# Feed-forward of an encoder trunk: when the activations' forms are cut, how early plain weights are begun, and which engine makes the activations' low halves

## The chip, the cores and the metric

One Trainium2 chip, one of its cores. The core has TensorE (PE: matrix products; PEld is its loading of the stationary operand), VectorE (DVE), ScalarE (ACT), GpSimd (POOL) and SyncE (SP), which issues most transfers. Each engine works through its own instructions in the order in which they were written; semaphores let one engine wait for another. The metric is device time of one execution in microseconds. The kernel before takes 1579.46 us (median of three runs, 1577.26 to 1580.77).

## The reference

Two layers of an encoder on 512 tokens of 1024 channels, in float32. The attention half of a layer (latent attention, grouped-query attention, pooling, gates) is untouched by the change. The feed-forward half is:

```python
hf = rms_norm(x, ffn_norm_g[l])
u = depthwise_conv(hf @ ffn_w_up[l], ffn_conv_w[l], ffn_conv_b[l])   # width 3, along the tokens
u_gate, u_val = u[..., :D_FF], u[..., D_FF:]                         # D_FF = 2816
x = x + (jax.nn.silu(u_gate) * u_val) @ ffn_w_down[l]
```

## The kernel before, in words

**Three products for one.** Every matrix is held as a rounded high half (type fp32r) and a low half, the rest. `mm3` makes a product of three matmuls: high by high, high by low, low by high. So everything that PE reads has to be cut into two halves first: ACT copies the value into the high tile, and the low tile is the value less the high one.

**How a low half is made.** For plain weights of the feed-forward ("u", line 436) and for the forms "11", "12" and "22" the function `by_transfer` does it: ACT writes the high half (`wh`, `fh`) and its negative (`wl`, `fl`), and a transfer on POOL's queue adds the raw weight to that. For the other forms, and for the activations' forms, DVE subtracts. For the finished activation of a chunk (`ah`/`al`, or `HH`/`HL` where the tile is kept in the place of the normalised input) the subtraction was POOL's (line 1675).

**The feed-forward's chunks.** The 2816 hidden channels are 22 chunks of 128 channels, each with a gate part and a value part, in groups of 6, 5, 4, 4 and 3 (`SIZES`). The first group (chunks 0 to 5) is computed plainly: 12 units, of 24 matmuls of 512 columns each. The other chunks go by a scheme with seven products in place of eight, on halves of the tokens and four-way splits of the inputs: per chunk seven forms in the order 11, 12, 1, 22, 2, 4, 3 (`FORMS`), each 12 matmuls of 256 columns (four input pieces q, by three). After the forms 22, 2, 4 and 3 stand matmuls of the down projection of earlier groups ("d", into `ps_mi` and `ps_S`). Each form needs its own combination of weights (`w_form`) and of the normalised input. The input's combinations are built once a layer by `build_forms`, during the plain chunks: eight normalised tiles `hn`, of them four times four sums `tt` (`sums`), and of `hn` and `tt` six sets of four tiles `tf` (`cut`), each one ACT copy (high) and one DVE subtraction (low). The tiles `tf` stay for all sixteen chunks of the layer.

**What sets the order.** One program text writes all engines. A clock (`Clock`) goes forward with each matmul written; a `chain` is a list of steps, each written when the clock's estimate says that the one before is done. So the order on DVE, ACT and POOL follows from when a step came due in that estimate, not from any priority on the chip. Before, the eight `hn` and the four `sums` are one chain without pause, and the `tf` come in two chains beside each other:

```python
chain(*[lambda k=k: normed(k) for k in range(KC)], *[lambda q=q: sums(q) for q in range(4)], after=0.0)
for names in (("11", "1", "2"), ("12", "22", "3")):
    chain(*[z for name in names for q in range(4) for z in cut(name, q)], after=0.3)
```

**When weights are begun.** `wnext` gives PE's next piece of weights, and ahead of that begins the cutting of pieces `n` further on: `LA` = 3 among plain pieces, `LAF` = 6 near forms. Raw weights come by SP's queue into tiles of 1024 columns for a pair of pieces, or, for the four inputs of a form, into single slots ("alone"). `room` says how many of each kind may be held at once: 3 pairs and 8 alone. A new transfer is written when a tile comes free (`w_free`).

**The end of a chunk.** `convolve` takes the finished `u`: an ACT step with scale and bias (`a<-u,prm`), two DVE steps for the neighbours (`a<-u,prm,a`), for the gate part a Silu on ACT (`a<-a,a` on DVE for the product with the value part), then the cut into high and low.

Of the kernel before, what the change touches and what calls it, by code (L numbers as in the profile page):

```python
# [19 lines left out]
T = 512  # L20
D = 1024
KC = D // P
# [10 lines left out]
RAW = 3  # L33
ALONE = 8
# [5 lines left out]
MID = 5  # L40
PRE_A = 16
PRE_B = 8
LA, LAF = 3, 6
SIZES = (6, 5, 4, 4, 3)
PLACE = {1: 0, 2: 5, 3: 0}
KEEP = 2
FORMS = ("11", "12", "1", "22", "2", "4", "3")
SPOTS = ("22", "2", "4", "3")
END = object()
# [142 lines left out]
class Clock:  # L192
# [37 lines left out]
    def done(self, *key):  # L230
        self.ready[key] = self.fin + self.SEM
# [7 lines left out]
    def has(self, *keys):  # L239
        return all(self.ready.get(k, 1e9) <= self.now for k in keys)  # L240

    def chain(self, *steps, after=0.2):

        def go(n, source=None):
            if n == len(steps):
                return
            keys, fn = steps[n] if isinstance(steps[n], tuple) else ((), steps[n])
            late = [self.ready.get(k, self.now + 0.5) for k in keys]
            if late and max(late) > self.now:
                self.at(max(late) - self.now, lambda: go(n))  # L250
                return
            self.fin, self.source, self.last = self.now, source, None
            fn()
            source, self.source = self.last, None
            self.at(max(0.0, self.fin - self.now), lambda: go(n + 1, source))
        self.at(after, lambda: go(0))

    def drain(self):
# [63 lines left out]
def trunk(ctx: ExitStack, tc: tile.TileContext, x, w, prm, gb, cst, out):  # L322
# [3 lines left out]
    at, need, done, chain = ck.at, ck.need, ck.done, ck.chain  # L326
    V, A, G = Engine(ck, nc.vector, "DVE"), Engine(ck, nc.scalar, "ACT"), Engine(ck, nc.gpsimd, "Pool")
# [54 lines left out]
    st = {"dma": 0, "split": 0, "use": 0, "ffn": False}  # L382
    raws, halves, second = {}, {}, {}
    kinds = [2 if i < KC else int(a) for i, a in enumerate(alone)]
    held, room = [0, 0, 0], (RAW, ALONE, KC)

    def w_dma():
        i = st["dma"]
# [6 lines left out]
    def w_until(i):  # L395
        while st["dma"] <= min(i, len(swidth) - 1):
            w_dma()
# [52 lines left out]
    def w_form(j, form, pi):  # L450


        sl = [pieces[pi + n][0] for n in range(4)]
        w_until(sl[3])
        a11, a12, a21, a22 = (raws[i][:, :T] for i in sl)
        ck.fin = ck.now
        if form in ("11", "12", "22"):
            hi, lo = halves[j] = pair(j, True)
            by_transfer(hi[:, :T], lo[:, :T], {"11": a11, "12": a12, "22": a22}[form])
            done("w", j)  # L460
            return
        hi, lo = halves[j] = pair(j)
        if form == "2":
            second[pi] = slot("s2")[:, :T]
        s2 = second.get(pi)
        dst, x, y, op, keys, gone = {
            "1": (a21, a21, a22, ALU.add, [], None),
            "2": (s2, a21, a11, ALU.subtract, [("sum", pi, "1")], 0),
            "4": (a12, a12, s2, ALU.subtract, [("sum", pi, "2")], None),
            "3": (s2, a22, s2, ALU.subtract, [("sum", pi, "4"), ("form", pi, "2")], 3)}[form]  # L470

        def total():
            V.tensor_tensor(dst, x, y, op)
            done("sum", pi, form)
            if gone is not None:
                w_free(sl[gone])

        def low():
            V.tensor_tensor(lo[:, :T], dst, f(hi[:, :T]), ALU.subtract)
            done("w", j)  # L480
            done("form", pi, form)
            if form == "4":
                w_free(sl[1])
            if form == "2":
                w_free(sl[2])

        chain((keys, total), lambda: A.activation(hi[:, :T], dst, AF.Copy), low, after=0.0)
# [10 lines left out]

    def wnext():
        j = st["use"]  # L500
        n = LAF if any(units[min(i, len(units) - 1)][0] not in "pu" for i in (j, j + LAF)) else LA
        w_ahead(j + n if j > LA else j)
        st["use"] += 1
        need(("w", j))
        return halves.pop(j)
# [35 lines left out]
    def split(hi, lo, src, scale=None, eng=None):  # L541

        steps = []
        if scale is None:
            steps.append(lambda: A.activation(hi, src, AF.Copy))
            steps.append(lambda: (eng or V).tensor_tensor(lo, src, f(hi), ALU.subtract))
        else:
            steps.append(lambda: A.activation(hi, src, AF.Copy, scale=scale))
            steps.append(lambda: V.scalar_tensor_tensor(lo, src, scale, f(hi), ALU.mult, ALU.subtract))
        return steps  # L550
# [116 lines left out]
    def layer(l, sq, xsrc):  # L667
# [927 lines left out]
        def build_forms():  # L1595
            for q in range(4):
                m = mp.tile([P, 3, T], F32R, tag="m", name=f"tf{l}{q}")
                forms["raw", q] = m
                for n, name in enumerate(("11", "12", "4")):
                    forms[name, q] = m[:, n, :]  # L1600
                for name in ("1", "22", "2", "3"):
                    forms[name, q] = slot("tf", F32R)[:, :T]
            hn, tt = {}, {}
            lo, hi = slice(0, 256), slice(256, 512)

            def normed(k):
                hn[k] = slot("hn")[:, :T]
                V.scalar_tensor_tensor(hn[k], XM[:, k, :], col(PRM_FG + k), fin["rbc"][:, :T], ALU.mult, ALU.mult)
                done("hn", l, k)

            def sums(q):
                a, b = hn[2 * q], hn[2 * q + 1]
                t = tt[q] = (slot("tt")[:, :T], slot("tt")[:, :T])
                V.tensor_tensor(t[0][:, lo], a[:, hi], a[:, lo], ALU.subtract)
                V.tensor_tensor(t[1][:, lo], b[:, hi], a[:, hi], ALU.subtract)
                V.tensor_tensor(t[0][:, hi], b[:, hi], t[0][:, lo], ALU.subtract)
                V.tensor_tensor(t[1][:, hi], b[:, lo], t[0][:, hi], ALU.subtract)
                done("tt", l, q)

            def cut(name, q):  # L1620
                n = "tt"
                if name == "11":
                    src, dh, dl, n = lambda: hn[2 * q][:, lo], forms[name, q][:, lo], forms[name, q][:, hi], "hn"
                elif name == "12":
                    m = forms["raw", q]
                    src, dh, dl, n = (lambda: hn[2 * q + 1].rearrange("p (a b) -> p a b", a=2)), m[:, 1:3, lo], m[:, 1:3, hi], "hn"
                else:
                    i, h = {"1": (0, lo), "2": (0, hi), "3": (1, lo), "22": (1, hi)}[name]
                    src, dh, dl = lambda: tt[q][i][:, h], forms[name, q][:, lo], forms[name, q][:, hi]

                def low():
                    V.tensor_tensor(dl, src(), f(dh), ALU.subtract)
                    done("tf", l, name, q)
                    if name == "12":
                        done("tf", l, "4", q)
                key = ("tt", l, q) if n == "tt" else ("hn", l, 2 * q + (name == "12"))
                return [([key], lambda: A.activation(dh, src(), AF.Copy)), low]

            chain(*[lambda k=k: normed(k) for k in range(KC)], *[lambda q=q: sums(q) for q in range(4)], after=0.0)
            for names in (("11", "1", "2"), ("12", "22", "3")):  # L1640
                chain(*[z for name in names for q in range(4) for z in cut(name, q)], after=0.3)

        chain(([("rbc", G2)], build_forms), after=3.0)

# [10 lines left out]
        def convolve(c, part, u):  # L1655
            ci = c + part * FC
            a = slot("a")
            steps = [
                lambda: A.activation(a[:, :T], u[:, :T], AF.Identity, bias=col(PRM_B + ci),
                                     scale=col(PRM_W1 + ci)),  # L1660
                lambda: V.scalar_tensor_tensor(a[:, 1:T], u[:, 0:T - 1], col(PRM_W0 + ci), a[:, 1:T],
                                               ALU.mult, ALU.add),
                lambda: V.scalar_tensor_tensor(a[:, 0:T - 1], u[:, 1:T], col(PRM_W2 + ci), a[:, 0:T - 1],
                                               ALU.mult, ALU.add)]
            if part == 0:
                def gate():
                    A.activation(a[:, :T], a[:, :T], AF.Silu)
                    gated[c] = a
                    done("gate", l, c)
                return steps + [gate]  # L1670
            ah, al = act[c] = keep_act(c)

            def prod():
                V.tensor_tensor(a[:, :T], a[:, :T], gated.pop(c)[:, :T], ALU.mult)
            return steps + [([("gate", l, c)], prod), *split(ah, al, a[:, :T], eng=G), lambda: done("act", l, c)]

        def plain(c, part):
            n = 2 * c + part
# [328 lines left out]
```

## Time and profile before

| | |
|---|---|
| median of the runs | 1579.46 us |
| profiled execution | 1578.39 us |
| its span | 1576.6 us |
| PE busy | 1548.2 us, 98% |
| DVE, ACT, POOL busy | 70%, 66%, 55% |

How to read a profile line: a start and a duration in us, the engine, the source line, the operation, then what is written and what is read by the program's names (`wl<-raw`), partitions x elements. In brackets stands the idle time of that engine just before, and what ended it. In a table of windows the columns are: the window and its length, then for PE, PEld, DVE, ACT and POOL the busy time and in brackets the number of instructions, then the granted TensorE clock (1.00 is full), the share of the transfer engines' time (it can come out above 1) and GB/s. The plain stage of the first layer runs from 432.45 us to 502.81 us, the first chunk with forms (chunk 6) follows it. The second layer repeats this 781.3 us later.

### The profile page before, as it was taken

What the parts mean: (1) busy time and instruction counts of PE and PEld (TensorE: products, weight loads), DVE (VectorE), ACT (ScalarE), POOL (GpSimd) and SP (SyncE); (2) the same over time, 40 slices, a digit from 0 to 9 for tenths busy, and PEclk for the clock granted to TensorE, in tenths of its full rate; (3) what the DMA queues carried; (4) which work ended last, traced back from release to release, by engine and by line L of the source; (5) the groups of instructions that cost most, each with busy time, mean ns of one, the idle gap of its engine ahead of it and who ended that gap; (6) DMA issues with size and microseconds to landing.
All of it is one profiled execution on the core that took longest, in us unless ns stands there. A gap on an engine that the chain in (4) does not pass through costs nothing.

```text
span 1576.6 us, 23997 instructions
## 1 busy us (share of the span) xinstructions
PE 1548.2 (98%) x8193; PEld 1338.6 (85%) x8193; DVE 1111.4 (70%) x1816; ACT 1034.4 (66%) x1932; POOL 859.7 (55%) x868
## 2 busy tenths in 40 slices
PE   9999989999999999999999999899999999999999
PEld 8888878888877999998888888788888779999987
DVE  6867886875278777777656688778652877777774
ACT  5557776763478777777655587666535787777773
POOL 3974876854653433333588658668546443333333
PEclk9999999999999999999999999999999999999999
DMA  5432224324489887886535322343244798888853
GB/s 205 126 114 74 74 85 144 107 67 134 113 179 230 200 193 185 205 183 132 135 117 141 100 74 74 96 138 101 70 146 123 170 229 192 192 198 187 194 113 101
DMA packets 127563, 222.36 MB, mean 141 GB/s; under 512 B 29648, under 2 KB 51664, under 8 KB 127440
## 3 DMA queue, kind: packets, MB, share of 16 engines
q1 hardware_dynamic: 90864, 162.93, 33.2%
q0 software_dynamic: 31680, 57.69, 21.3%
q8 instruction: 64, 1.05, 0.3%
q10 hardware_dynamic: 4896, 0.21, 0.2%
q14 instruction: 59, 0.48, 0.1%
HBM read 149.41 MB, written 13.63 MB: 103 GB/s over the span
## 4 chain that ended last, share of the span: by engine, by line
PE 74%; DVE 13%; ACT 6%; issue 4%; POOL 2%; DMA 1%; SPq 0%; ACTq 0%; DVEq 0%; POOLq 0%
PE ps_acc L508 32%; PE ps_AV L508 14%; PE ps_ST L508 12%; PE ps_S L508 8%; PE ps_mi L508 8%; DVE a L294 2%; DVE XM L290 2%; ACT wh L283 1%; DVE wl L290 1%; DVE u L290 1%; DVE mgl L290 1%; ACT mgh L283 1%; DVE hn L294 1%; ACT fh L283 1%; DVE tf L290 1%
## 5 line engine op out<-in xcount | busy, mean ns | idle before, releaser
L290 POOL TENSOR_TENSOR wl<-raw,wh 128x512 fp32r<-128x512 f32 (+3 forms) x241 | 305.0, 1275 | 224.6 <-ACT wh L283 206.5
L283 ACT ACTIVATE wh<-raw 128x512 fp32r<-128x512 f32 (+2 forms) x457 | 269.2, 605 | 56.9 <-DVE raw L290 12.9
L421 POOL DMA_DIRECT2D wl<-raw x124 | 110.9, 919 | 290.3 <-ACT wl L283 106.0
L508 PE MATMUL ps_acc<-HH,wl 128*128 128x512 f32 x416 | 164.3, 395 | 6.2 <-DMA wl<-raw 6.2
L508 PE MATMUL ps_acc<-HH,wh 128*128 128x512 f32 x416 | 164.1, 394 | 3.4 <-DVE vm L290 2.9
L294 DVE SCALAR_TENSOR_TENSOR a<-u,prm,a 128x511 f32<-128x511 f32 x176 | 142.8, 811 | 32.2 <-ACT a L283 31.2
L508 PE MATMUL ps_acc<-HL,wh 128*128 128x512 f32 x416 | 163.5, 393 | 0.0
L421 POOL DMA_DIRECT2D fl<-raw x96 | 85.2, 887 | 105.7 <-ACT sx L283 47.0
L290 DVE TENSOR_TENSOR wl<-raw,wh 128x512 fp32r<-128x512 f32 (+2 forms) x93 | 92.4, 995 | 60.6 <-ACT wh L283 60.5
L283 ACT ACTIVATE a<-u,prm 128x512 f32<-128x512 f32 x88 | 71.5, 815 | 86.6 <-DVE u L290 86.2
L298 DVE TENSOR_REDUCE nm<-ps_S 128x1 fp32r<-128x512 f32 x128 | 87.6, 685 | 36.0 <-PE ps_S L508 34.8
L508 PEld LDWEIGHTS ps_acc<-HH,wl 128*128 128x128 f32 x416 | 78.8, 189 | 24.9 <-DMA wl<-raw 7.9
L508 PEld LDWEIGHTS ps_acc<-HH,wh 128*128 128x128 f32 x416 | 79.0, 190 | 19.8 <-issue 4.4
L508 PE MATMUL ps_AV<-tf,wh 128*128 128x256 f32 x512 | 94.8, 283 | 0.0
L508 PE MATMUL ps_acc<-tf,wh 128*128 128x256 f32 x512 | 94.4, 282 | 0.0
L508 PE MATMUL ps_ST<-tf,fh 128*128 128x256 f32 x512 | 94.2, 281 | 0.0
L508 PEld LDWEIGHTS ps_acc<-HL,wh 128*128 128x128 f32 x416 | 78.9, 190 | 16.3
L508 PEld LDWEIGHTS ps_acc<-tf,wh 128*128 128x128 f32 x512 | 83.9, 191 | 5.3
L508 PEld LDWEIGHTS ps_AV<-tf,wh 128*128 128x128 f32 x512 | 81.4, 190 | 2.6
L283 ACT ACTIVATE wl<-wh 128x512 fp32r<-128x512 f32 x124 | 78.5, 633 | 3.9
L508 PEld LDWEIGHTS ps_ST<-tf,fh 128*128 128x128 f32 x512 | 79.4, 190 | 0.0
L508 PE MATMUL ps_acc<-tf,wl 128*128 128x256 f32 x256 | 72.4, 283 | 0.0
(417 smaller groups left out, 4844.8 us busy)
## 6 DMA issues: line engine op xcount, KB each, us to landing
raw<-w SPq DMA_DIRECT2D x162, 512.0 KB, 3.7
raw<-w SPq DMA_DIRECT2D x136, 256.0 KB, 4.2
wl<-raw POOLq DMA_DIRECT2D x124, 256.0 KB, 4.3
fl<-raw POOLq DMA_DIRECT2D x96, 256.0 KB, 5.4
raw<-w SPq DMA_DIRECT2D x14, 384.0 KB, 3.0
XM<-x SPq DMA_DIRECT2D x16, 256.0 KB, 3.2
dtq<-tr SPq DMA_DIRECT2D x16, 192.0 KB, 1.9
dtk<-tr SPq DMA_DIRECT2D x16, 192.0 KB, 2.0
```

Of the source, the lines that this page charges most:

```text
L283: return self.eng.activation(out, in_, func, **k)
L290: return self.eng.tensor_tensor(out, *a)
L294: return self.eng.scalar_tensor_tensor(out, *a)
L298: return self.eng.tensor_reduce(out, in_, *a, **k)
L421: nc.gpsimd.dma_start(f(lo), r, accum_op=ALU.add)
L508: PE.matmul(o, lhsT=lhsT, rhs=rhs, start=start, stop=stop, skip_group_check=again)
```

## The change

Four edits, none of which changes a value that is computed:

- `build_forms`: `hn` and `tt` are now built four times in the row hn, hn, sums, with at least 1.9 us between the starts of steps (`PACE_H`), and the `tf` in one chain in the order in which PE uses them (11, 12, 1, 22, 2, 3), with at least 1.0 us between steps (`PACE_F`). A step is one ACT copy or one DVE subtraction.
- `wnext`: between plain pieces of the feed-forward, cutting begins 4 pieces ahead (`LAP`) in place of 3.
- `room`: at first, and until a form comes up within the next 24 units, 4 alone raws may be held in place of 8. (One chunk's forms use four.)
- `convolve`: the low half of an activation is POOL's for chunks 0 to 4 and DVE's from chunk 5 on, 17 in each layer.

```diff
-LA, LAF = 3, 6
+LA, LAP, LAF = 3, 4, 6
+PACE_H, PACE_F = 1.9, 1.0
@@ class Clock
-    def chain(self, *steps, after=0.2):
+    def chain(self, *steps, after=0.2, pace=0.0):
...
-            self.at(max(0.0, self.fin - self.now), lambda: go(n + 1, source))
+            self.at(max(pace, self.fin - self.now), lambda: go(n + 1, source))
@@ trunk
-    held, room = [0, 0, 0], (RAW, ALONE, KC)
+    held, room = [0, 0, 0], [RAW, 4, KC]
@@ w_form
         sl = [pieces[pi + n][0] for n in range(4)]
+        room[1] = ALONE if any(u[0] not in "pu" for u in units[j + 1:j + 24]) else 4
         w_until(sl[3])
@@ wnext
-        n = LAF if any(units[min(i, len(units) - 1)][0] not in "pu" for i in (j, j + LAF)) else LA
+        kinds_ = [units[min(j + i, len(units) - 1)][0] for i in (0, LAP, LAF)]
+        n = LAF if any(k not in "pu" for k in kinds_) else LAP if "u" in kinds_[:2] else LA
@@ build_forms
-            chain(*[lambda k=k: normed(k) for k in range(KC)], *[lambda q=q: sums(q) for q in range(4)], after=0.0)
-            for names in (("11", "1", "2"), ("12", "22", "3")):
-                chain(*[z for name in names for q in range(4) for z in cut(name, q)], after=0.3)
+            chain(*[z for q in range(4) for z in (lambda q=q: normed(2 * q), lambda q=q: normed(2 * q + 1), lambda q=q: sums(q))],
+                  after=0.0, pace=PACE_H)
+            chain(*[z for name in FORMS if name != "4" for q in range(4) for z in cut(name, q)], after=0.3, pace=PACE_F)
@@ convolve
-            return steps + [([("gate", l, c)], prod), *split(ah, al, a[:, :T], eng=G), lambda: done("act", l, c)]
+            return steps + [([("gate", l, c)], prod), *split(ah, al, a[:, :T], eng=G if c < SIZES[0] - 1 else V), lambda: done("act", l, c)]
```

The orders of PE and of SP stay the same, row for row. Three places on the other engines, with the rows as they stand in the two programs (numbers behind a name tell tiles of one name apart; they differ between the programs):

ACT, first layer, inside chunk 6, where PE works on its forms 1, 22 and 2; `fh` and `fl` are chunk 7's first weight forms. Before, no `tf` stands here, since all are cut:

```order
L283 ACTIVATE wh_5353<-s_824_5281 128x512
L283 ACTIVATE wh_5376<-raw_5208 128x512
L283 ACTIVATE wl_5377<-wh_5376 128x512
L283 ACTIVATE sx_5307<-ps_AV_5352 128x256
L283 ACTIVATE ah_5302<-a_5301 128x512
L283 ACTIVATE fh_5395<-raw_5210 128x512
```

Now (`tf_4744` and `tf_4749` are the pieces q = 2 and 3 of form 2, `tf_4735` is q = 0 of form 3):

```order
L284 ACTIVATE wl_5364<-wh_5363 128x512
L284 ACTIVATE tf_4744<-tt_4929 128x256
L284 ACTIVATE sx_5294<-ps_AV_5340 128x256
L284 ACTIVATE ah_5289<-a_5288 128x512
L284 ACTIVATE fh_5384<-raw_5166 128x512
L284 ACTIVATE fl_5385<-fh_5384 128x512
L284 ACTIVATE sx_5294<-ps_ST_5362 128x256
L284 ACTIVATE fh_5399<-raw_5168 128x512
L284 ACTIVATE fl_5400<-fh_5399 128x512
L284 ACTIVATE tf_4749<-tt_4990 128x256
L284 ACTIVATE tf_4735<-tt_4793 128x256
```

The last piece of form 2 is now cut five rows behind the place of the first `fh`, in the chunk whose own form 2 reads it.

DVE a little further on, where the first sum of down products has to be added to `XM`. Before:

```order
L290 TENSOR_TENSOR s_849_5468<-raw_5214,raw_5210 128x512
L290 TENSOR_TENSOR XM<-ps_mi_5400,XM 128x512
L294 TENSOR_SCALAR a_5452<-u_5304,prm_91,a_5452 128x511
L290 TENSOR_TENSOR wl_5467<-s_849_5468,wh_5466 128x512
L290 TENSOR_TENSOR u_5305<-ps_acc_5308,sx_5307 128x256
```

Now (`tf_4745` and `tf_4750` are the pieces q = 2 and 3 of form 3):

```order
L291 TENSOR_TENSOR XM<-ps_mi_5389,XM 128x512
L295 TENSOR_SCALAR a_5446<-u_5291,prm_91,a_5446 128x511
L291 TENSOR_TENSOR tf_4745<-tt_4930,tf_4745 128x256
L291 TENSOR_TENSOR wl_5463<-s_849_5464,wh_5462 128x512
L295 TENSOR_SCALAR a_5446<-u_5291,prm_91,a_5446 128x511
L291 TENSOR_TENSOR tf_4750<-tt_4991,tf_4750 128x256
```

Two low halves that PE's form 3 reads now stand behind the step that waits for the last matmul ahead of form 3 (`XM<-ps_mi`).

POOL in chunk 18 of the first layer, before: the low half of that chunk's activation stands behind two transfers of weights.

```order
L421 DMA wl_7952<-raw_7599 128x512
L421 DMA fl_7998<-raw_7713 128x512
L421 DMA fl_8018<-raw_7737 128x512
L290 TENSOR_TENSOR HL<-a_7913,HH 128x512
L421 DMA fl_8058<-raw_7793 128x512
```

Now it is DVE's:

```order
L291 TENSOR_TENSOR a_7914<-a_7914,a_7877 128x512
L291 TENSOR_TENSOR wl_7975<-s_1126_7894,wh_7974 128x512
L291 TENSOR_TENSOR HL<-a_7914,HH 128x512
L291 TENSOR_TENSOR raw_7769<-raw_7769,raw_7795 128x512
L291 TENSOR_TENSOR wl_8032<-raw_7769,wh_8031 128x512
```

It follows the product that it cuts by one row, and stands ahead of the next chunk's first sum of weights.

## The prediction

> **What bounds the kernel.** I read the page first (busy shares), then the chain of what PE waits for, then windows over the feed-forward's stages, then PE's, ACT's, DVE's and POOL's timelines around each wait.
>
> ```profile
> span 1576.6 us, 23997 instructions
> PE 1548.2 (98%) x8193; PEld 1338.6 (85%) x8193; DVE 1111.4 (70%) x1816; ACT 1034.4 (66%) x1932; POOL 859.7 (55%) x868
> ...
> PE ps_acc L508 <- DMA wl<-raw: 6.2, 3, 3.0
> PE ps_mi L508 <- POOL HL L290: 4.6, 2, 2.4
> ...
> PE ps_ST L508 <- DMA wl<-raw: 1.6, 2, 0.9
> ...
> PE ps_mi L508 <- POOL al L290: 0.2, 1, 0.2
> ```
>
> PE is busy for 98% of the span. The change adds and removes no matmul, so it can only touch the 28.4 us in which PE stands (1576.6 less 1548.2) and the time at a lowered clock. The rows (total, times, longest) name what it could touch: waits for weights' low halves, 7.8 us, and for POOL's low halves of activations, 4.8 us. Where they lie, and what they do to the clock:
>
> ```profile
> 432.45:502.80 70.35, 66.43 (x291) 54.06 (x290) 54.99 (x96) 53.28 (x97) 34.37 (x32) 1.00 0.87 201
> 1213.70:1286.80 73.10, 69.16 (x291) 56.02 (x291) 56.51 (x97) 53.46 (x97) 34.69 (x33) 0.95 0.86 203
> 484.00:488.00 4.00, 1.48 (x7) 1.03 (x6) 3.86 (x8) 3.34 (x7) 0.88 (x1) 1.00 1.09 293
> 1268.00:1272.00 4.00, 3.89 (x9) 3.12 (x10) 1.97 (x5) 3.91 (x9) 2.63 (x3) 0.50 1.11 247
> 726.00:730.00 4.00, 1.85 (x13) 1.76 (x14) 2.98 (x2) 1.76 (x4) 2.98 (x3) 1.00 1.02 225
> 1512.80:1516.20 3.40, 3.40 (x15) 3.11 (x14) 0.92 (x2) 0.84 (x2) 0.00 (x0) 0.51 0.90 163
> 486.79 0.50 PE L508 MATMUL ps_acc<-HH,wl 128*128 128x512 f32 x1 [2.52 <-DMA wl<-raw]
> 1268.11 0.80 PE L508 MATMUL ps_acc<-HH,wl 128*128 128x512 f32 x1 [2.96 <-DMA wl<-raw]
> 728.15 0.50 PE L508 MATMUL ps_mi<-HL,wh 128*128 128x512 f32 x1 [2.25 <-POOL HL L290]
> 1511.82 0.50 PE L508 MATMUL ps_mi<-HL,wh 128*128 128x512 f32 x1 [2.37 <-POOL HL L290]
> ```
>
> The first two rows are the plain stage of each layer. PE is idle 70.35 − 66.43 = 3.9 us in the first and 73.10 − 69.16 = 3.9 in the second. The second is 2.75 us longer at the same idle time: its wait of 2.96 us is followed by a granted clock of 0.50, the shorter wait of 2.52 us in the first layer is not (1.00 in its window). Of POOL's two waits the one of 2.37 us is followed by 3.4 us at 0.51, which costs half of that, 1.7 us, the one of 2.25 us by none. So in reach are 3.9 us and 6.7 us in the plain stages (3.9 + 2.75), and 2.3 us and 4.1 us (2.37 + 1.7) at POOL's waits: 17 us, 1.1% of the time.
>
> **POOL's low halves go to DVE.**
>
> ```profile
> 723.74 0.62 ACT L283 ACTIVATE HH<-a 128x512 fp32r<-128x512 f32 x1
> 726.52 1.58 POOL L290 TENSOR_TENSOR HL<-a,HH 128x512 fp32r<-128x512 f32 x1
> 726.37 2.29 DVE L290 TENSOR_TENSOR wl<-raw,wh 128x512 fp32r<-128x512 f32 x1 [2.57 <-ACT wh L283]
> ```
>
> The high half is there at 724.36, but POOL stands at transfers of weights that are written ahead of it and begins at 726.52. PE wanted the tile at 728.15 − 2.25 = 725.9. DVE is idle for 2.57 us before 726.37, thus from 723.8 on, and in its new place `HL` comes ahead of that row. On DVE a subtraction of 512 columns takes some 0.68 us (the row of `XM` below), so it is done by about 725.2. The wait goes: −2.3 us in the first layer, −4.1 in the second. The 0.2 us for `al` goes too. Seventeen times 0.68 us more on DVE per layer lie in the chunks with forms, where DVE is busy 70% over the span. Bounds: no cost, or a few tenths where DVE is the last to deliver (it is in chunk 6, costed below); I take none elsewhere.
>
> **Weights a piece earlier.** A plain piece serves PE for 12 matmuls of 0.228 us (66.43 over 291), 2.7 us. Four pieces ahead begin each low half's transfer 2.7 us sooner. That is as long as the wait at 486.79 and longer than the small ones. Against it: around that wait the transfer engines are full (share 1.09 at 484 to 488 us), because the four raws for chunk 6 come then, and SP's order has not changed with `room`. Bounds for the stage's gain: 0 and 3.9 us in the first layer, 0 and 6.7 in the second; the edit to `room` is costed at nothing, as no row of SP moves (which slots tiles share may still move, and with them a wait of SP: some tenths either way).
>
> **Forms in spread steps.** This is where I expect the gain to be lost. Now 14 of the 24 ACT copies `tf` stand behind chunk 4's gate step, and the last eight inside chunk 6 itself, in the row in which ACT and DVE also make that chunk's weights.
>
> ```profile
> 502.81 0.40 PE L508 MATMUL ps_acc<-tf,fh 128*128 128x256 f32 x2
> 510.99 0.40 PE L508 MATMUL ps_acc<-tf,wh 128*128 128x256 f32 x2
> 511.35 0.40 PE L508 MATMUL ps_mi<-ah,wh 128*128 128x512 f32 x1
> 1295.38 0.40 PE L508 MATMUL ps_mi<-ah,wh 128*128 128x512 f32 x1
> 486.31 0.71 ACT L283 ACTIVATE tf<-tt 128x256 fp32r<-128x256 f32 x2
> 492.19 0.71 ACT L283 ACTIVATE tf<-tt 128x256 fp32r<-128x256 f32 x2
> 492.80 0.81 ACT L283 ACTIVATE a<-u,prm 128x512 f32<-128x512 f32 x1
> 508.68 0.37 ACT L283 ACTIVATE sx<-ps_acc 128x256 f32<-128x256 f32 x1
> 511.51 0.62 ACT L283 ACTIVATE fh<-raw 128x512 fp32r<-128x512 f32 x1
> 514.16 0.37 ACT L283 ACTIVATE sx<-ps_acc 128x256 f32<-128x256 f32 x1
> 492.80:511.51 18.71, 18.71 (x112) 16.70 (x112) 17.44 (x27) 14.45 (x27) 7.63 (x8) 1.00 1.00 263
> L283 ACT ACTIVATE tf<-tt 128x256 fp32r<-128x256 f32 x32 | 11.8, 403 | 0.2
> L290 DVE TENSOR_TENSOR tf<-tt,tf 128x256 fp32r<-128x256 f32 x32 | 12.4, 418 | 7.7 <-ACT tf L283 7.7
> ```
>
> Chunk 6 begins on PE at 502.81; the last piece of its form 2 begins at 510.99, 8.2 us later, and the down products at 511.35. ACT is behind PE here already: it copies out the first form at 508.68, though that form's 12 short matmuls began at 502.81. So what stands in ACT's row is late by what is ahead of it, not by PE.
>
> When is the low half of the last piece of form 2 (`tf_4749`) ready? Five steps.
> 1. Chunk 4's gate step `a<-u,prm`, at 492.80 before. At the latest it stays. At the earliest it comes by all of the stage's idle time (3.9) and by the four `tf` copies just ahead of it that are now elsewhere (0.71 twice): 487.5. I take the middle, 490.15.
> 2. From there to the place of the first `fh` it was 18.71 us, with DVE busy for 17.44 of them. Now six more low halves (0.42 each) and one `al` (0.68) are DVE's in that stretch, 3.2 us. At the least they are all hidden (0), at the most none (3.2); I take 3.2 less DVE's 1.27 idle us, 1.9.
> 3. Five ACT rows more stand ahead of it (`fh`, `fl`, `sx`, `fh`, `fl`): 514.16 − 511.51 = 2.65 us.
> 4. Its own copy and subtraction, 0.40 + 0.42 us.
> 5. PE's remaining matmuls of the piece, 0.4 us.
>
> 490.15 + 18.71 + 1.9 + 2.65 + 0.82 = 514.2, and the down products begin at 514.6, against 511.35: **+3.3 us** in the first layer. In the second the stage starts 781.3 us later, which gives 1295.9 against 1295.38: **+0.5 us**. Both already hold whatever the plain stage gains, since PE arrives early and waits: at 507.1 to 511.0 (8.2 us behind a chunk that starts up to 3.9 us sooner), a wait of 3 to 7 us. The bounds of the steps give 510.1 to 518.6, thus −1.2 to +7.2 in the first layer and −4.0 to +4.5 in the second.
>
> Form 3 is next, and its wait is in the order itself:
>
> ```profile
> 516.03 0.39 PE L508 MATMUL ps_acc<-tf,wh 128*128 128x256 f32 x2
> 516.82 0.68 DVE L290 TENSOR_TENSOR XM<-ps_mi,XM 128x512 f32<-128x512 f32 x1
> 517.42 0.74 DVE L294 SCALAR_TENSOR_TENSOR a<-u,prm,a 128x511 f32<-128x511 f32 x1
> ```
>
> DVE can begin `XM` only when the last down matmul ends, which is when form 3 begins on PE. Behind it stand a step of 0.74 us, the low half for q = 2, two more steps and the low half for q = 3. From 516.82 to 517.42 a step of 0.68 takes 0.60 of the queue, 0.08 less than its duration; so 0.60, 0.66, 0.34, 0.60, 0.66 and the whole 0.42 make 3.3 us from the down matmuls' end to the last low half. PE wants it after three pieces of 0.36 (510.99 to 511.35), about 1.1. A wait of **+2.2 us** per layer; bounds 0, if PE comes to form 3 late for a reason ahead of it that DVE doesn't share, and 2.4, with 0.2 for the hand-over from PE.
>
> **Clock after the new waits.** Waits of 2.25 and 2.52 us left the clock at 1.00, those of 2.37 and 2.96 us cost 1.7 and 2.75 us more. The new ones are 3 to 7 us. Bounds per layer 0 and 2.75; I take 1.5, because the slow stretch would fall on form 3's wait, where PE has to stand anyway: **+3** for both. The Trainium skill, "TensorE: Matmul & The Clock Gate", Part 1 "The HAM clock gate", says that the clock is halved after an idle window of about 3.4 us, which runs free of the program; the 2.37 us wait here lowered it as well, so 3.4 us is no safe bound in this trace. By the rule alone every wait longer than 3.4 us would be followed by one whole slow window, an estimate of 1.7 us per layer, +3.4 in place of +3.
>
> **Sum.** First layer 3.3 + 2.2 − 0.2 − 2.3 + 1.5 = +4.5; second 0.5 + 2.2 − 4.1 + 1.5 = +0.1; together +4.6 us. The profiled execution took 1578.39 us (span 1576.6 and 1.8 around it), so 1583.0; the median of the runs is 1.07 above it: **1584 us**, 0.3% slower. A measurement of this kernel tells about 0.2%, 3.2 us, from no change. With all steps at their lower bounds (and form 3's wait kept) the sum is −1.2 − 4.0 + 4.4 − 0.2 − 2.3 − 4.1 = −7.4, 1572; at the upper ones 7.2 + 4.5 + 4.8 − 0.2 − 6.4 + 5.5 = +15.4, 1595.
>
> **Rivals.**
> A, faster: the forms are in time in chunk 6. Place: form 2's last piece; it decides when that low half is ready by 507.1, when PE arrives with the plain stage's waits gone. For it: two DVE steps in that stretch are stretched beside POOL, which DVE then hasn't to bear if POOL's work shifts.
>
> ```profile
> 496.76 1.78 DVE L294 SCALAR_TENSOR_TENSOR a<-u,prm,a 128x511 f32<-128x511 f32 x1
> 501.02 2.46 DVE L294 SCALAR_TENSOR_TENSOR a<-u,prm,a 128x511 f32<-128x511 f32 x2 [0.28 <-ACT a L283]
> ```
>
> Against 0.74 undisturbed they lose 1.0 and 1.0 us. With step 1 at 487.5, the stretch at 16.7 and step 2 at 0 the piece is ready at 507.7, nearly in time. Against it: the low halves of chunks 3 and 4, which lie beside those steps, stay on POOL, and all three must hold. Gains then 3.9 + 6.7 + 2.3 + 4.1 + 0.2 = 17.2, less 4.4 for form 3: 1567 us.
> B, no change: step 1 and 2 between middle and lower bound, `tf_4749` ready at about 512, no low clock: +1 in the first layer, −1.7 in the second, 4.4 for form 3, −6.6 for POOL's waits: −2.9, 1577 us.
> C, clearly slower: the transfers at 484 to 488 us are as late as before, since they lie beside the same four raws. Then step 1 stays at 492.80 and the waits in chunk 6 come on top of those in the plain stage, with two stretches of half clock per layer: toward the upper sum, 1592 us.
> D, the weights edit does nothing because ACT's row, not the due time, sets when a piece is cut. Step 1 then is 2.65 us later in both layers with the other terms in the middle, 1589 us.
>
> **Chances.** My forecast, D beside it, 0.47; A 0.2; B 0.21; C 0.12. The range reaches from A to beyond C: 1567 to 1593. Faster by over 0.2%: A and half of B, 0.3; within: the other half and the near side of the forecast, 0.2; slower: 0.5.
>
> **What would show it.** Right: a wait of PE for `tf` (by DVE, or ACT) of 3 to 7 us before the down products of chunk 6 in both layers; one of about 2 us in form 3; no wait for POOL's `HL`; plain stages of 66 to 70 us. Wrong: no PE wait for `tf` at all (A), a wait for `wl<-raw` of over 2 us still in the plain stages (C), or waits for DVE in later chunks because of `al` and `HL`, which I cost at nothing.

## The result and the profile after

The changed kernel takes 1595.13 us (median of 4 runs, 1594.52 to 1596.62) against 1578.36 us of the kernel before in the same session: a ratio of 1.0109, 95% interval 1.0088 to 1.0131. It is 17 us slower. The forecast was 1584 us, slower, with a range up to 1593 us. The profiled execution took 1595.41 us. From its page, and what PE waits for (total, times, longest):

```profile
span 1593.6 us, 23976 instructions
PE 1558.2 (98%) x8193; PEld 1347.1 (85%) x8193; DVE 1106.8 (69%) x1850; ACT 1035.6 (65%) x1932; POOL 809.7 (51%) x834
...
PE ps_acc L511 <- ACT tf L284: 6.9, 4, 2.5
PE ps_acc L511 <- DMA wl<-raw: 5.2, 2, 2.6
PE ps_acc L511 <- ACT sx L284: 4.2, 2, 2.2
PE ps_acc L511 <- DVE tf L291: 3.9, 4, 1.0
```

POOL's rows are gone from the waits, as the 34 instructions less on POOL and more on DVE should make it. The weights' transfers cost 5.2 us where they cost 7.8. New are 15.0 us of waits for `tf` and for copies out of form 11's sum, `sx`. PE is also busy 10 us longer with the same 8193 matmuls, at a mean granted clock of 0.989 where it was 0.997.

PE's timeline of the first layer, each row with the idle time before it: the plain stage's one large wait, form 2 in chunk 6, the down products behind it, form 3.

```profile
484.83 0.80 PE L511 MATMUL ps_acc<-HH,wl 128*128 128x512 f32 x1 [2.62 <-DMA wl<-raw]
511.83 0.76 PE L511 MATMUL ps_acc<-tf,wh 128*128 128x256 f32 x2 [2.25 <-ACT sx L284]
514.40 1.04 PE L511 MATMUL ps_acc<-tf,wh 128*128 128x256 f32 x2 [0.95 <-ACT tf L284]
518.12 1.04 PE L511 MATMUL ps_acc<-tf,wh 128*128 128x256 f32 x2 [2.47 <-ACT tf L284]
519.17 0.63 PE L511 MATMUL ps_mi<-ah,wh 128*128 128x512 f32 x1
526.66 0.39 PE L511 MATMUL ps_acc<-tf,wh 128*128 128x256 f32 x1 [0.95 <-DVE tf L291]
528.26 0.38 PE L511 MATMUL ps_acc<-tf,wh 128*128 128x256 f32 x1 [0.98 <-DVE tf L291]
```

And the granted clock there, third number from the right, in windows of 4 us:

```profile
484.00:488.00 4.00, 3.17 (x8) 2.50 (x9) 3.48 (x6) 3.23 (x7) 1.72 (x2) 0.57 1.09 275
510.00:514.00 4.00, 1.61 (x6) 1.32 (x6) 3.96 (x8) 3.49 (x9) 0.88 (x1) 0.74 0.27 47
514.00:518.00 4.00, 1.26 (x3) 0.79 (x3) 1.18 (x3) 3.94 (x11) 1.74 (x2) 0.50 0.66 129
518.00:522.00 4.00, 3.88 (x11) 3.13 (x12) 2.06 (x4) 2.73 (x7) 0.87 (x1) 0.50 1.03 217
528.00:532.00 4.00, 3.74 (x11) 3.04 (x12) 2.46 (x6) 2.61 (x5) 0.00 (x0) 0.62 0.16 59
```

PE's order is the same in both kernels, so the start of a matmul in one trace less its start in the other shows where time came or went. Starts taken from PE's timelines:

| place on PE | first layer, before → after | so far | second layer, before → after | so far | from the layer's start |
|---|---|---|---|---|---|
| chunk 6 begins | 502.81 → 502.32 | −0.5 | 1286.85 → 1294.07 | +7.2 | −3.0 |
| down products behind form 2 | 511.35 → 519.17 | +7.8 | 1295.38 → 1310.62 | +15.2 | +5.0 |
| form 4, behind them | 512.73 → 521.73 | +9.0 | 1296.77 → 1313.18 | +16.4 | +6.2 |
| down products behind form 3 | 517.45 → 528.60 | +11.2 | 1301.00 → 1320.23 | +19.2 | +9.0 |
| chunk 7 begins | 519.52 → 532.11 | +12.6 | 1303.07 → 1323.54 | +20.5 | +10.3 |
| behind chunk 18's activation | 728.72 → 738.91 | +10.2 | 1516.75 → 1533.37 | +16.6 | +6.4 |

(The second layer starts 10.2 us late.) In each layer, counted from where chunk 6 begins, form 2 costs some 8 us, the half clock behind it 1.2, form 3 2.2 to 2.8 with the clock beside it, and the half clock behind that 1.2 to 1.4. What the activations' low halves give back is 2.4 and 3.9.

### The profile page after: what moved, and what is told of

Same layout as the page of the kernel before. It is cut to its first block, busy times and chain, and to the rows that moved or that the text cites. A ratio compares the mean times of both kernels' runs of the same rounds, so it can differ in the third digit from the quotient of the medians.

```text
span 1593.6 us, 23976 instructions
## 1 busy us (share of the span) xinstructions
PE 1558.2 (98%) x8193; PEld 1347.1 (85%) x8193; DVE 1106.8 (69%) x1850; ACT 1035.6 (65%) x1932; POOL 809.7 (51%) x834
## 4 chain that ended last, share of the span: by engine, by line
PE 80%; DVE 11%; ACT 4%; issue 2%; POOL 1%; DMA 1%; SPq 0%; ACTq 0%; DVEq 0%; POOLq 0%
PE ps_acc L511 33%; PE ps_AV L511 15%; PE ps_ST L511 13%; PE ps_S L511 10%; PE ps_mi L511 9%; DVE a L295 3%; DVE XM L291 1%; DVE tt L291 1%; DVE tf L291 1%; ACT wh L284 1%; DVE mgl L291 1%; ACT mgh L284 1%; DVE u L291 1%; DMA XM<-x 1%; DVE hn L295 1%
## 5 line engine op out<-in xcount | busy, mean ns | idle before, releaser
L295 DVE SCALAR_TENSOR_TENSOR a<-u,prm,a 128x511 f32<-128x511 f32 x176 | 139.2, 791 | 34.7 <-ACT a L284 33.0
L511 PE MATMUL ps_acc<-tf,wh 128*128 128x256 f32 x512 | 99.4, 290 | 15.0 <-ACT tf L284 6.9
L291 DVE TENSOR_TENSOR wl<-raw,wh 128x512 fp32r<-128x512 f32 (+2 forms) x93 | 68.9, 742 | 45.6 <-ACT wh L284 45.6
```

The costliest lines, as they stand in the source:

```text
L291: return self.eng.tensor_tensor(out, *a)
L295: return self.eng.scalar_tensor_tensor(out, *a)
L511: PE.matmul(o, lhsT=lhsT, rhs=rhs, start=start, stop=stop, skip_group_check=again)
```

## The experiments

Theory 1: the whole loss comes from the forms' spread steps, and the cause is where in ACT's and DVE's rows the last of them stand; the other edits gain. Rivals: the other edits share the loss, by crowding the same engines in chunk 6; or it is the length of the pauses as such. Times are medians; the ratio is to runs of the kernel before beside them (1578.6 to 1579.6 us). The waits and windows of all runs are from one profiled execution each.

**Each edit alone, and all but the forms.**

Low halves of chunks 5 and up on DVE, nothing else:

```diff
 before
-*split(ah, al, a[:, :T], eng=G)
+*split(ah, al, a[:, :T], eng=G if c < SIZES[0] - 1 else V)
```

> Before with one edit alone: the low halves of activations from chunk 5 on are made by DVE. Theory 1 (the whole loss comes from cutting the forms in spread steps, and this edit only gains): PE's waits of 2.4 and 2.5 us for POOL's HL and the 0.4 for al are gone, with the half clock after the second, so some 6.5 us less than before: about 1572 us. Rival (DVE is too full in chunk 6, and this edit is part of what makes the forms late): 1578 us or more, with waits of PE for DVE in chunk 6.

Measured 1571.49 us, ratio 0.9955 (0.9939 to 0.9971): −7.5 us (1571.49 − 1578.96), as theory 1 had it.

The forms' chains alone:

```diff
 before
-chain(*[... normed ...], *[... sums ...], after=0.0)
-for names in (("11", "1", "2"), ("12", "22", "3")):
-    chain(*[... cut(name, q)], after=0.3)
+chain(*[... normed, normed, sums per q ...], after=0.0, pace=PACE_H)
+chain(*[... cut(name, q), names in FORMS' order], after=0.3, pace=PACE_F)
```

> Before with one edit alone: hn, sums and tf built in spread steps. Theory 1: the changed kernel loses in chunk 6 of the two layers some 13 us each (form 2 about 8.2, form 3 about 2.2, half clock behind both about 2.6), and nothing else there adds to it: 1578 + 26 = 1604 us, 1600 to 1608. Rival (the loss needs the other edits too: al on DVE and weights begun earlier in the same row of ACT and DVE): less than half of it, 1583 to 1591 us.

Measured 1602.17 us, ratio 1.0152 (1.0132 to 1.0173): +23 us (1602.17 − 1578.96). Of the four edits the forms' alone makes the loss; no other is needed for it.

The changed kernel with the two old chains:

```diff
 changed
-chain(*[... normed, normed, sums per q ...], after=0.0, pace=PACE_H)
-chain(*[... cut(name, q), names in FORMS' order], after=0.3, pace=PACE_F)
+chain(*[... normed ...], *[... sums ...], after=0.0)
+for names in (("11", "1", "2"), ("12", "22", "3")):
+    chain(*[... cut(name, q)], after=0.3)
```

> The changed kernel with the forms built as before (two chains without pause); weights four pieces ahead, room of four alone at first, and DVE's low halves stay. Theory 1: no wait in forms 2 and 3, the gain of DVE's low halves (6.5) and that of the plain stages (0.5 and 3.0 in the changed kernel's trace) remain: about 1568 us, 1565 to 1572. Rival (the other edits share the loss): 1578 us or more.

Measured 1569.90 us, ratio 0.9947 (0.9930 to 0.9964). Without the forms' edit the change would have been 9 us faster than the kernel before.

Weights four pieces ahead, with the room of four:

```diff
 before
+LAP = 4
-n = LAF if any(...) else LA
+n = LAF if any(...) else LAP if "u" in kinds_[:2] else LA
-room = (RAW, ALONE, KC)
+room = [RAW, 4, KC]     # ALONE again near forms
```

> Before with two edits alone: plain weights begun four pieces ahead, and room for four alone raws at first. Theory 1: the plain stages get 0.5 and 3.0 us shorter, as in the changed kernel's trace, so about 1575 us; its largest wait for a transfered low half stays at 2.5 to 2.8 us, since that transfer still lies beside the four alone raws. Rival a (those 3.5 us came from the forms' spread steps, which leave ACT freer in the plain stage): 1578 us, no change. Rival b (four pieces ahead do what they are for): all 10.6 us of the plain stages' idle time and low clock, 1568 us.

Measured 1575.72 us, ratio 0.9982 (0.9970 to 0.9993), the time of theory 1, but not by its account. The largest wait for a `wl` transfer fell to 0.9 us, against the 2.5 to 2.8 expected, and the matmul that stands at 491.93 us in the first layer before comes 3.1 us sooner. Most of it is then lost to waits that were not there before:

```profile
PE ps_mi L510 <- POOL al L290: 3.3, 2, 1.7
...
PE ps_ST L510 <- DMA fl<-raw: 2.4, 4, 1.1
PE ps_mi L510 <- POOL HL L290: 2.1, 2, 1.2
PE ps_acc L510 <- DMA wl<-raw: 1.9, 4, 0.9
```

PE comes earlier and meets POOL's `al` (3.3 us where it was 0.2) and the forms' weights `fl`. So the 2.62 us that the changed kernel still waits in the plain stage are of the spread steps' making too: without them the longest such wait is 0.8 us (all but the forms) or 0.9 us (this run), with the same start four pieces ahead.

**Which part of the forms' edit.**

No pause between the steps of `tf`:

```diff
 changed
-PACE_H, PACE_F = 1.9, 1.0
+PACE_H, PACE_F = 1.9, 0.0
```

> The changed kernel with no pause between the steps of tf (one chain in PE's order stays, hn and sums stay spread). ACT then cuts the last piece of form 2 fourteen rows sooner, ahead of the copies out of form 11's sum, and DVE's last low half for form 3 stands ahead of the step that waits for the down matmuls. Theory 1 (what costs is how late these rows stand): form 3's waits (2.2 us a layer) are gone, form 2's are 0 to 2 us, and the time is 1568 to 1576 us. Rival (the tf rows hold ACT and DVE up by turns wherever they stand beside the weights of chunk 6): form 2 still waits 4 us or more, 1580 us or more.

Measured 1572.74 us, ratio 0.9961 (0.9946 to 0.9976). Form 3's waits are gone; in form 2 of the first layer a wait of 2.0 us for `sx` stays.

`hn` and sums at once, `tf` with the pause:

```diff
 changed
-chain(*[... normed, normed, sums per q ...], after=0.0, pace=PACE_H)
+chain(*[... normed ...], *[... sums ...], after=0.0)
```

> The changed kernel with hn and sums built at once as before, and tf in one chain with 1.0 us steps. The last piece of form 2 stands on ACT where it stands without the pause (fourteen rows sooner than in the changed kernel). Theory 1: as that kernel, 1568 to 1576 us; neither pause alone makes the forms late, the two together do. Rival (the 1.0 us pause alone does it): as the changed kernel, 1590 to 1597 us.

Measured 1572.66 us, ratio 0.9964 (0.9951 to 0.9977). Each pause alone is nearly free: both of these kernels take some 3 us more than the one with all forms as before (1569.90), and the next run, with `hn` spread too, does not, so most of that goes with the one chain for `tf`. Both pauses together cost 22 us more. In both of these runs the last copy of form 2 stands fourteen rows sooner on ACT than in the changed kernel, where the later sums and the slower cutting add up until the last rows fall behind chunk 6's own work. Here one wait is left in form 3, 1.1 us in the first layer and 0.3 us in the second.

`tf` in the two old chains, `hn` and sums spread:

```diff
 changed
-chain(*[... cut(name, q), names in FORMS' order], after=0.3, pace=PACE_F)
+for names in (("11", "1", "2"), ("12", "22", "3")):
+    chain(*[... cut(name, q)], after=0.3)
```

> The changed kernel with tf in the two chains of before, without pause; hn and sums stay spread. All tf rows stand ahead of chunk 6's first copy out of a sum. Theory 1: no wait in forms 2 and 3; as the kernel with all forms as before, about 1570 us (1567 to 1573). If spread hn leave ACT freer for the weights in the plain stages, 1 to 3 us less than that one.

Measured 1569.23 us, ratio 0.9943 (0.9927 to 0.9959): the same as with all forms as before. Spreading `hn` gives nothing that these runs can tell.

**Place in the row, or length of the pause.** Pauses of 0.9 and 0.8 us in place of 1.0, same edit as above with those numbers:

> The changed kernel with 0.9 in place of 1.0 us between the steps of tf. ACT cuts the last piece of form 2 six rows sooner; two low halves of form 3 still stand behind the step that waits for the down matmuls. Theory 1 (place in the row decides): form 2's waits fall from 7 us by the six rows' 2.5 to 3 us, to some 4 us; form 3's two waits of 1.1 us stay; half clock 1 to 2.5 us. Per layer 7 to 9 us over the kernel with forms as before (1569): 1583 to 1588 us. Rival (it is the length of the pauses as such): a tenth less pause, a tenth less loss, 1592 us.

> The changed kernel with 0.8 us between the steps of tf. ACT cuts the last piece of form 2 ten rows sooner than in the changed kernel, and all of form 3's low halves stand ahead of the step that waits for the down matmuls. Theory 1 (place in the row decides): form 3's waits are gone, form 2's are 1 to 3 us, no or one short half clock: 1572 to 1579 us. Rival (length of the pauses): 1588 to 1591 us.

Measured 1582.28 us (ratio 1.0029, 1.0018 to 1.0040) and 1574.27 us (0.9971, 0.9962 to 0.9981). A pause of 1.0, 0.9, 0.8 and 0 us gives 1595, 1582, 1574 and 1573 us: 13 us for the first tenth, 8 for the second, 1.5 for the other eight. The time goes by rows: the last copy of form 2 stands six rows sooner at 0.9, ten at 0.8, fourteen at 0. At 0.9 two low halves still stand behind `XM`, and two pieces of form 3 still wait (1.6 and 1.0 us); form 2's waits came out shorter than expected, 1.7 and 0.4 us in the two layers against some 4. At 0.8 no low half stands behind `XM`, yet one wait of 0.7 us per layer is left in form 3, where I had expected none. The run with 0.9 came out 0.7 us under theory 1's span.

**Form 3's term alone.**

```diff
 changed
-chain(*[... cut(name, q), names in FORMS' order], after=0.3, pace=PACE_F)
+chain(*[... cut("3", q)], after=0.3)
+chain(*[... cut(name, q), the other names], after=0.3, pace=PACE_F)
```

> The changed kernel with form 3's tf cut in a chain of their own without pause, so that all of them stand well ahead of the down matmuls; form 2's stay as late as they are. It measures form 3's term alone. Theory 1: the two waits of 1.1 us per layer are gone, and of the half clock behind them 0 to 1.4: 1595 - 2 x (2.2 to 3.6) = 1588 to 1591 us; form 2's waits stay at 6 to 8 us. Rival (form 3 waits only because DVE is late from form 2 on): form 3 waits elsewhere, 1594 us or more.

Measured 1588.45 us, ratio 1.0068 (1.0047 to 1.0089): 6.7 us less than the changed kernel, 3.3 per layer, the size of form 3's two waits and most of the half clock behind them. PE doesn't wait in form 3 at all, so the order itself had made that wait. Form 2 still waits, 4.9 us in the first layer (5.7 in the changed kernel, 6 to 8 expected), and form 22 ahead of it now waits 1.1 us.

**The edit to room.**

```diff
 changed, forms as before
-room = [RAW, 4, KC]
-room[1] = ALONE if any(...) else 4
+room = [RAW, ALONE, KC]
```

> The kernel with forms as before, weights four pieces ahead and DVE's low halves, but with room for eight alone raws throughout as before. It shows what the edit to room is worth, whose rows on SP do not move. Theory 1 (nothing): 1570 us. Rival (the room decides when raws are fetched and so what the low halves' transfers lie beside): a wait of over 2 us for a transferred low half is back in a plain stage, 1573 to 1576 us.

Measured 1568.52 us, ratio 0.9936 (0.9920 to 0.9951). No loss without it: the edit is worth nothing that can be told.

**The low halves of chunks 0 to 4.**

```diff
 changed, forms as before, room for eight
-eng=G if c < SIZES[0] - 1 else V
+eng=V
```

> The best so far (forms as before, four pieces ahead, room for eight) with the low halves of chunks 0 to 4 on DVE too. In the plain stages DVE's steps beside POOL's subtractions took 2 to 2.5 us in place of 0.74; with POOL's gone they should not. Theory 1: the plain stages and chunk 6 gain 0 to 1.5 us each, 1566 to 1569 us. Rival (DVE is full there, 0.68 us five times more): 1570 us or more, with waits for DVE in the plain stage or chunk 6.

Measured 1559.49 us, ratio 0.9879 (0.9864 to 0.9894): 19 us faster than before and 9 less than the kernel with POOL's five subtractions a layer, where I had expected 1566 to 1569 us. No wait for a transfer is left among PE's waits. The two groups that changed, in the first plain stage (432.45 to 502 us; count, then busy time and mean ns of one), with POOL's subtractions (the kernel before this edit, room for eight):

```profile
L295 DVE SCALAR_TENSOR_TENSOR a<-u,prm,a 128x511 f32<-128x511 f32 x20 | 17.6, 881 | 0.3 <-ACT a L284 0.3
L291 POOL TENSOR_TENSOR al<-a,ah 128x512 fp32r<-128x512 f32 x5 | 9.8, 1968 | 0.6 <-ACT ah L284 0.6
```

and without:

```profile
L295 DVE SCALAR_TENSOR_TENSOR a<-u,prm,a 128x511 f32<-128x511 f32 x22 | 16.4, 747 | 0.4 <-ACT a L284 0.3
L291 DVE TENSOR_TENSOR al<-a,ah 128x512 fp32r<-128x512 f32 x5 | 3.4, 685 | 0.1
...
432.45:498.00 65.55, 65.55 (x292) 54.31 (x291) 51.83 (x100) 52.29 (x95) 25.86 (x27) 1.00 0.87 206
```

The last row is the window of the plain stage: PE is busy for all of its 65.55 us at full clock.

**The changed kernel with all low halves on DVE.** Same one-word edit, on the changed kernel as it is:

> The changed kernel, spread steps and all, with the low halves of chunks 0 to 4 on DVE too, so that no POOL subtraction of an activation lies beside the stretch in question. Theory a (DVE's steps of 2.55 and 2.10 us beside POOL, 3.2 us over 0.74 each, are most of the excess of 4.4): form 2's piece is ready 3 us sooner, 1595 - 2 x 3 to 4 = 1587 to 1589 us. Theory b (the tf rows make ACT and DVE wait by turns): the stretch stays at 22 us or more, since DVE has 0.68 us twice more to do there, and PE, which comes sooner, waits longer in form 2: 1592 to 1596 us.

Measured 1581.72 us, ratio 1.0016 (1.0005 to 1.0026): 13.4 us less than the changed kernel, more than theory a asked for. No wait for a weight's transfer is left among PE's waits. In form 2 one wait of 2.8 us per layer stays, and form 3's two are as before (0.95 and 0.97 us). ACT's two rows that bound the stretch, DVE's step in it, and the window:

```profile
487.88 0.80 ACT L284 ACTIVATE a<-u,prm 128x512 f32<-128x512 f32 x1
507.75 0.62 ACT L284 ACTIVATE fh<-raw 128x512 fp32r<-128x512 f32 x1
497.72 0.75 DVE L295 SCALAR_TENSOR_TENSOR a<-u,prm,a 128x511 f32<-128x511 f32 x1 [0.29 <-ACT a L284]
487.88:507.75 19.87, 18.79 (x103) 15.76 (x102) 17.86 (x32) 16.58 (x34) 4.92 (x6) 1.00 0.96 247
```

**The same without the earlier start.** On the fastest kernel:

```diff
 forms as before, room for eight, all low halves on DVE
-LA, LAP, LAF = 3, 4, 6
+LA, LAP, LAF = 3, 3, 6
```

> The fastest kernel so far (forms as before, all low halves on DVE, 1559.5 us) with plain weights begun three pieces ahead as before. Theory a (POOL's subtractions in the plain stage made the transfers late, by POOL's queue and by DVE's stretched steps): no wait of over 1 us for a transferred low half, 1559 to 1562 us. Theory b (the earlier start does it): the waits of 2.5 and 3.0 us of before are back, with half clock behind one: 1565 to 1570 us.

Measured 1565.00 us, ratio 0.9904 (0.9885 to 0.9923). Between the two theories: the long waits of before are not back (the longest for a `wl` transfer is 1.2 us), so POOL's subtractions had made those; but some 4 to 5.5 us are the earlier start's (by the two ratios, or by the two medians). Where in the chunks they lie was not taken apart.

## Why the prediction was wrong

The way was right, the size was not: +4.6 us forecast, +17 measured. The result came at the prediction's own upper sum (1595 us), which its range, ending at 1593, had left out. What failed is step 2 of form 2's piece, the length of the stretch on ACT in which the new rows stand. Step by step:

- **POOL's low halves to DVE** (−2.3, −4.1, −0.2). Right: −2.4 and −3.9 by the table, −7.5 by the edit alone. The cost "none elsewhere" held.
- **Weights a piece earlier** (bounds 0 to 3.9 and 0 to 6.7, not counted in the sum, since PE arrives early in chunk 6 and waits). Right as bounds: the plain stages gained 0.5 and 3.0, and chunk 6 took them back. But rival C's sign came: a wait for `wl<-raw` of over 2 us in both plain stages (2.62 and 2.61), half clock behind it, and chunk 6's waits on top. C, given a chance of 0.12 and 1592 us, was the rival that came nearest. Its reason does not hold, since the four raws alone don't make that transfer late: with the forms as before the longest wait is 0.8, and with POOL's subtractions gone there is none. `room`, costed at nothing, is worth nothing.
- **Form 2's piece** (+3.3 and +0.5). This is the term that failed: +7.8 and +5.0, an excess of 4.5 us in each layer. Its five steps against the trace:

```profile
491.78 0.80 ACT L284 ACTIVATE a<-u,prm 128x512 f32<-128x512 f32 x1
515.03 0.62 ACT L284 ACTIVATE fh<-raw 128x512 fp32r<-128x512 f32 x1
517.67 0.70 ACT L284 ACTIVATE tf<-tt 128x256 fp32r<-128x256 f32 x2
518.10 0.76 DVE L291 TENSOR_TENSOR tf<-tt,tf 128x256 fp32r<-128x256 f32 x2 [2.24 <-ACT tf L284]
491.78:515.03 23.25, 20.05 (x110) 17.16 (x109) 20.27 (x31) 16.91 (x34) 7.73 (x9) 0.93 0.85 208
```

Step 1, the start at 490.15: it was 491.78, +1.6, only 1.0 ahead of its place before. Step 3, five rows of ACT, 2.65: 517.67 − 515.03 = 2.64. Step 4, the piece's own 0.82: 518.10 + 0.42 − 517.67 = 0.85. Step 5, 0.4: 519.17 − 518.52 = 0.65, at half clock.

Step 2, the stretch, is the one that failed: 18.71 + 1.9 = 20.6 was forecast, 21.9 at most, and 23.25 came. I had DVE's 3.2 us of new work first use up its 1.27 us of idle time, and gave ACT's new copies no time at all. The windows show the contrary on both engines. ACT, in whose row the place lies, is busy for 16.91 us, 2.5 more than before (14.45), mostly by six copies `tf` more; and it stands for 6.3 us, 2.1 more than before. DVE is busy for 20.27 us, 2.8 more, and idle for 2.98, 1.7 more. (Chunk 5's `al`, which I had counted in the 3.2, does not fall in the stretch; DVE makes it at 515.16.) Each engine waits for the other: a low half on DVE can't begin before ACT has come to its copy, behind the weights, and two of ACT's rows wait for DVE's two longest, the second by way of the sum `s` that stands behind it:

```profile
493.62 2.55 DVE L295 SCALAR_TENSOR_TENSOR a<-u,prm,a 128x511 f32<-128x511 f32 x1
493.99 1.61 POOL L291 TENSOR_TENSOR al<-a,ah 128x512 fp32r<-128x512 f32 x1
502.91 0.43 DVE L291 TENSOR_TENSOR tf<-tt,tf 128x256 fp32r<-128x256 f32 x1 [1.25 <-ACT tf L284]
503.54 1.62 POOL L291 TENSOR_TENSOR al<-a,ah 128x512 fp32r<-128x512 f32 x1
503.62 2.10 DVE L295 SCALAR_TENSOR_TENSOR a<-u,prm,a 128x511 f32<-128x511 f32 x1 [0.28 <-ACT a L284]
496.20 0.63 ACT L284 ACTIVATE a<-a 128x512 f32<-128x512 f32 x1 [1.82 <-DVE a L295]
506.41 0.63 ACT L284 ACTIVATE wh<-s 128x512 fp32r<-128x512 f32 x1 [2.52 <-DVE s L291]
```

The prediction held the two long DVE rows against a faster rival ("low halves of chunks 3 and 4 stay on POOL") but not as a part of the size. With POOL's subtractions gone, the stretch is 19.87 us and starts at 487.88, by the rows of the changed kernel with all low halves on DVE: 3.4 us less in step 2 and 3.9 in step 1, together more than the excess. So the excess hangs on POOL's subtractions in the plain stage, since with the last `tf` at the same place in ACT's row it is gone. In step 2 they act by DVE's long rows: without them DVE is busy 2.4 us less, with an `al` of 0.68 us more to make, and ACT stands for 3.3 us in place of 6.3, which is nearly all of the 3.4. In step 1, whether they act by such rows or by the transfers that stand behind them on POOL's queue, the runs don't separate.

Each long DVE row lies beside one of POOL's subtractions: a step begun at 493.62 ends at 496.17, one begun at 503.62 at 505.72, where POOL's end at 495.60 and 505.16. The Trainium skill, "SBUF — State Buffer", section "Who interferes with whom", says that a DVE instruction with two inputs in SBUF contends with a GpSimd instruction that reads SBUF, and that the one issued later is blocked. The rows agree that the two contend (2.55 and 2.10 us beside POOL, 0.75 for the row at 497.72 with POOL's subtraction gone); which was issued first they don't tell, since DVE's start is shown 0.37 us ahead of POOL's in the first pair and 0.08 behind it in the second, and DVE is the longer one in both.

- **Form 3** (+2.2 per layer). Right: two waits of 0.95 and 0.98 us with the matmuls they hold up, 2.2 and 2.8 with clock by the table, gone when the rows stand earlier (form 3's chain of its own).
- **Half clock** (+1.5 per layer). Low: 1.2 behind form 2 and 1.4 and 1.2 behind form 3, 2.6 and 2.5 per layer. I had argued that the slow stretch falls where PE waits anyway; one part did (form 2's matmuls between 514 and 518 us), the rest fell on down products that had nothing to wait for. The upper bound of 2.75 held.
- **The sum**: the two excesses, 2 × 4.5 and 2 × 1.1, are 11.2 of the 12.4 us between 4.6 and 17.
- **What would show it**: the waits in form 2 and form 3 came as written (5.7 us of idle time in form 2's three rows, of which 2.25 were for `sx`, a wait that I had not named), and so did the sign of rival C. No wait for `al` or `HL` came in later chunks. The range was too narrow above: even the upper sum of +15.4 took step 2 at 3.2 more than before, where it came to 4.5.

## What to carry to other kernels

In this kernel, pauses that spread a chain of work cost little (at most some 3 us) until its last rows fell behind work that the consumer needed at the same time. Then they cost more than their own length: with the last step of the pause, from 0.9 to 1.0 us, six ACT rows of 3.2 us moved ahead of form 2's last copy, and the time rose by 6.4 us per layer. Before spreading, count the rows that land behind the first use, and move only as many as end ahead of it. And when a term rests on a stretch in which two engines hand pieces to each other, count the new rows of both in full, and don't let them fill the idle time first: here that idle time was waiting for the partner, and it grew.

## What the runs showed that I had not expected

Five subtractions of POOL's per layer, 1.97 us each in the first plain stage, were worth 9 us of the whole kernel when DVE made them in 0.685 us each (1568.52 to 1559.49 us): DVE's steps beside them fell from 881 to 747 ns on average, and PE's waits for transferred low halves (2.6, 1.9 and 1.1 us in sum by their groups in the trace of the kernel with room for eight) went to none. The profile had named the transfers as what PE waited for, not POOL's subtractions.

Waits of 2.6 us brought half clock (484 to 488 us at 0.57) in the changed kernel, where in the kernel before one of 2.52 us had not. The wait of 2.25 us ahead of form 2 was followed by a lowered clock too (0.74 from 510 to 514 us), where before one of 2.25 us for `HL` had left it at 1.00. In these traces no single length of wait divides the two cases.
